# Weight parts in pair tiles: where the two parts of a split weight start in a partition

## The chip, the cores and the metric

The kernel runs on one core of one Trainium2 chip. The metric is the device time of one execution in microseconds, the median of several runs. The profile is one further execution, recorded by the hardware profiler; its span is the time from its first to its last instruction.

## The reference

Two decoder layers work on one sequence of 512 positions, with a width of 2048, in float32.

```python
for i in range(DEPTH):
    mod = (c_act @ ada_w[i] + ada_b[i])[:, None, :]
    shift, scale, gate = jnp.split(mod, 3, axis=-1)
    h = rmsnorm(x, norm_g[i]) * (1.0 + scale) + shift
    if i % N_MIXERS == 0:
        y = retention_branch(h, positions, ret_w_in[j], ret_gn_g[j], ret_w_out[j])
    else:
        y = mla_branch(h, positions, mla_w_in[j], ..., mla_w_out[j])
    x = x + gate * y
return rmsnorm(x, final_norm_g)
```

Layer 1 is a retention layer of 8 heads: `h @ w_in` gives queries and keys (256 columns a head each), values and gates (512 columns a head each); the branch output, gated, goes through `w_out` (4096 by 2048). Layer 2 is latent attention of 16 heads: an input projection to two latents of 512, a rotary key and a gate, up-projections of the latents, causal softmax attention, and an output projection (2048 by 2048).

## The kernel before

Everything is held transposed or in rows in tiles of 128 partitions. To keep float32 accuracy at the fast matmul format, every weight and activation is split in two parts of that format: hi, a cast by ScalarE (line 137, or in place at lines such as 846 and 850), and lo, the remainder, a subtraction by VectorE (line 138; 848, 851). A product is then three matmuls, hi x hi, hi x lo and lo x hi (`mm3`, lines 163 to 165, and lines 806 to 808 and 905 in the steps named below). TensorE thus runs some 11,000 matmuls of at most 128 by 128 by 512. In this document a matmul with 512 moving columns is called wide, one with 256 narrow.

A weight's way is: SyncE issues its load into a raw tile (three buffers of tag `raw`, three of `own_r`), ScalarE writes hi, VectorE writes lo, TensorE multiplies, and the tiles are free again. The hi and lo tiles are two separate tiles, from two rings of three buffers each (tags `whi` and `wlo`); a new tile takes a buffer of its ring that has come free. In the seven-product steps every fourth pair comes instead from a single extra pair (`own_h`, `own_l` in layer 1; two buffers `bm` in layer 2). Some weights use other rings (`k4b`, `big`).

The steps that the change touches:
- `plain_steps`: an ordinary product with a weight, three matmuls a block. Queries and keys of heads 1, 6 and 7 of layer 1 use it, as does the gate of layer 2 (`g2_steps`), whose first three units are worked in halves of 256 columns (line 1651).
- `seven_steps`: a product by seven block products in place of eight, for values and gates of heads 1 to 7 (tiles `vg...`) and for the two latents of layer 2. The weight parts are the moving operand, the activations and sums of them the stationary one. Units 0 to 7 of the first half (`vg_0..`) make products x, s, z, y with an even tile e and an odd tile o; the units of the second half (`vg_1..`) make x (with o), y (with e) and s (with o), in this order.
- `seven_rows_steps`: the same for queries and keys of heads 2 to 5 (tiles `qk_0..`, `qk_1..`) and for part of layer 2's gate, with the weight parts as the stationary operand and 256 moving columns (line 905).
- `o1_unit` and `o2_unit`: the output projections of the two layers (lines 1387 and 2309), wide for the most part, with some narrow units at their ends.

The order of the work on each engine is written out by the main loop over `steps`: loads three units ahead on SyncE's queue, the preparation (hi, lo) of the unit after the current one, the matmuls, and what follows; `behind` ties each engine's instructions to its last one. Within a unit the building layer decides the order on VectorE and ScalarE by when tiles come free. Modulation sums (line 1089) run on VectorE in between.

Tiles stand in SBUF one after another. A 32-byte tile `spacer` and the size of `qn_s` are chosen in the kernel before such that the operands of all wide and narrow matmuls start 64 bytes past a multiple of 128 in their partition.

Of the kernel before, what the change touches and what calls it, by code (L numbers as in the profile page):

```python
# [49 lines left out]
def hybrid_trunk_kernel(  # L50
# [71 lines left out]
    mhalf = base.tile([P, NT], F32, name="mhalf")  # L122
# [17 lines left out]
    def load_w(parts, a, b, name, later=None, where=None):  # L140
# [12 lines left out]
        return hi, lo  # L153
# [70 lines left out]
    a_col = [base.tile([P, KD], F32, name=f"a_col{i}") for i in range(2)]  # L224
    b_col = [base.tile([P, KD], F32, name=f"b_col{i}") for i in range(2)]
    gate_c = [base.tile([P, KD], F32, name=f"gate_c{i}") for i in range(2)]
# [92 lines left out]
    def first_load(kind, u):  # L319

        cn = 512
        tags = (("k4b", 4), ("k4b", 4)) if kind == "g" else (("whi", 3), ("wlo", 3))
        raw = big(f"{kind}0_{u}_raw", F32) if u == 0 else base.tile(
            [P, 2, cn], F32, tag="raw", bufs=3, name=f"{kind}0_{u}_raw"
        )
        c0 = {"v": 4096, "g": 8192}.get(kind)
        for dst, src in qk_parts(0, u) if kind == "qk" else [(whole, rows(w_ret_in, u, 2, c0, cn))]:
            nc.sync.dma_start(dst(raw), src)

        def prepare():  # L330
            hl = [base.tile([P, 2, cn], F32R, tag=t, bufs=n, name=f"{kind}0_{u}_{t}{i}") for i, (t, n) in enumerate(tags)]
# [377 lines left out]
    lpp = lp.__enter__()  # L709

# [27 lines left out]
    def plain_steps(nu, kn, parts, cn, name, take, n, lhs, rhs, evac, seeded=False, **kw):  # L738
# [3 lines left out]
        def step(u):  # L742
# [39 lines left out]
    def turns(raw_tags, part_tags):  # L782
# [12 lines left out]

        return raw_tile, part_tiles

    def seven_steps(h, block, form, raw_tile, part_tiles, finish, rows):


# [14 lines left out]
        def step(second, u):  # L815
# [14 lines left out]
            def prepare():  # L830
                e, o = w["e"], w["o"]
                if not second:
                    eh, el = part_tiles([P, 2, T], f"{n}e")
# [5 lines left out]
                    oh, ol = part_tiles([P, 2, T], f"{n}o")  # L839
# [4 lines left out]
                else:  # L844
                    oh, ol = part_tiles([P, 2, T], f"{n}o")
# [3 lines left out]
                    eh, el = part_tiles([P, T], f"{n}e")  # L849
# [37 lines left out]
    def seven_rows_steps(name, load_half, acts, sums, raw_tile, part_tiles, finish, rows):  # L887
# [30 lines left out]
        def step(second, u):  # L918
# [12 lines left out]
            def prepare():  # L931
                e, o = w["e"], w["o"]
                if not second:
                    e0, e1, o0, o1 = (t[:, :, j * H : (j + 1) * H] for t in (e, o) for j in range(2))
                    eh, el = part_tiles([P, 2, T], f"{n}e")
# [5 lines left out]
                    oh, ol = part_tiles([P, 2, T], f"{n}o")  # L941
# [4 lines left out]
                else:  # L946
                    oh, ol = part_tiles([P, 2, T], f"{n}o")
# [4 lines left out]
                    eh, el = part_tiles([P, T], f"{n}e")  # L952
# [36 lines left out]
    def heads_steps(h):  # L989
# [25 lines left out]
        ((lambda: lpp, ("own_h", "own_l"), 1), *3 * ((lambda: base, ("whi", "wlo"), 3),)),  # L1015
# [142 lines left out]
    def retention(h, own, own2=None):  # L1158
# [146 lines left out]
    for h in (6, 7):  # L1305
# [6 lines left out]
            ),  # L1312
# [54 lines left out]
    def o1_unit(n, r, u, kn, cn, where=(("whi", 3), ("wlo", 3))):  # L1367
# [85 lines left out]
    def second_out():  # L1453
        outs(2, range(4))
        for b in range(4):
# [6 lines left out]
            {4: 2 * (("big", 16),), 5: 2 * (("big", 16),), 6: 2 * (("k4b", 4),)}.get(u, (("whi", 3), ("wlo", 3))),  # L1462
# [157 lines left out]

    def l2_tile(tag, bufs, name, shape=(P, T), dt=F32):
        return pools["l2"].tile(list(shape), dt, tag=tag, bufs=bufs, name=name)
# [14 lines left out]
    ga = g2_steps(0, seeded=True)  # L1637
# [105 lines left out]
    qn_s = base.tile([P, 32], F32, name="qn_s")[:, :NT]  # L1743
# [25 lines left out]
    def latent_parts(n, g_c):  # L1769
# [11 lines left out]
    turns2 = turns(  # L1781
        ((lambda: pools["l2"], "bw", 2), (lambda: base, "raw", 3)),
        ((lambda: pools["l2"], ("bm", "bm"), 2), *3 * ((lambda: base, ("whi", "wlo"), 3),)),
    )
# [85 lines left out]
    def unit_prepare(kind, pr, u):  # L1870
        raw = unit_raw.pop((kind, pr, u))
        cn, tags = (384, (("whi", 3), ("wlo", 3))) if kind == "uq" else (512, 2 * (("k4b", 4),))
        hi, lo = unit_parts[kind, pr, u] = [
            base.tile([P, 2, cn], F32R, tag=t, bufs=n, name=f"{kind}_{pr}_{u}_{i}") for i, (t, n) in enumerate(tags)
        ]
# [70 lines left out]
    def attend(h):  # L1946
# [13 lines left out]
        def exps(i):  # L1960
            n = (i + 1) * P
            if i == 0:
# [194 lines left out]
    for i, step in enumerate(steps):  # L2157
        if i == n_p:
            lp.__exit__(None, None, None)
            l1 = tc.tile_pool(name="l1", bufs=1)  # L2160
            pools["l1"] = l1.__enter__()
        if i == n_l2:
            l1.__exit__(None, None, None)
            l2 = tc.tile_pool(name="l2", bufs=1)
            pools["l2"] = l2.__enter__()
        with behind(S_):
# [92 lines left out]
    def o2_unit(r, u, kn, cn, where=None):  # L2259
        wt = load_w([(whole, rows(w_mla_out, u, kn, r * T, cn))], kn, cn, f"o2_w{r}_{u}", where=where)  # L2260
# [212 lines left out]
```

## Time and profile before

| what | value |
|---|---|
| median of 3 runs | 2149.7 us (2149.39 to 2150.03) |
| the profiled execution's own time | 2149.59 us |
| its span | 2147.8 us |
| TensorE busy | 2122.6 us, 99% |
| VectorE busy | 1675.3 us, 78% |
| ScalarE busy | 1056.7 us, 49% |
| mean granted TensorE clock | 0.998 |

In the profile's rows PE is the matmuls of TensorE, PEld its weight loads, DVE VectorE, ACT ScalarE, SP SyncE. A row of a timeline has the start and the length in us, the engine, the line, the tiles (out<-in, buffer numbers left out), the shape and the count of merged instructions; in brackets, the idle time before it and what ended it. A row of a group has count, busy us and mean ns. Matmuls overlap each other, so a matmul's length is longer than the distance to the next one's start.

### The profile page before, as it was taken

Reading aid. Unit: us, or ns where it says so; the run is one execution under the profiler, and the core shown is the slowest. Engines: PE = TensorE matmul, PEld = TensorE weight load, DVE = VectorE, ACT = ScalarE, POOL = GpSimd, SP = SyncE. Lnnn points to the kernel's source line nnn. Section 1 sums busy time; section 2 is a strip of 40 time slices with the busy share of each in tenths; the row PEclk is TensorE's granted clock in tenths of the full one; section 3 lists DMA queues with packets and bytes.
Section 4 is the critical chain, followed back from the end, with each engine's and each line's share of the span. In section 5 each row is a group of like instructions: output and inputs, shape, how many; then the busy total and the mean of one; then the engine's idle time right before and its main releaser. Section 6 shows DMA issues by size and latency. Waiting matters only on the chain.

```text
span 2147.8 us, 30042 instructions
## 1 busy us (share of the span) xinstructions
PE 2122.6 (99%) x11100; PEld 1824.9 (85%) x11100; DVE 1675.3 (78%) x2482; ACT 1056.7 (49%) x1604; POOL 106.5 (5%) x178
## 2 busy tenths in 40 slices
PE   7999999999999999999999999999999999999998
PEld 5887898988889888888888888898889989988887
DVE  7899788888878789766777777668978788886745
ACT  5764444444444444434344544445446565664434
POOL 1000000000000000000000000010001000000000
PEclk9999999999999999999999999999999999999999
DMA  9976687877777778755647566553456644346734
GB/s 381 395 281 197 225 277 229 275 241 259 255 259 259 237 235 283 261 181 185 237 155 246 185 207 240 169 176 115 159 189 203 187 128 147 118 133 221 244 109 137
DMA packets 229782, 462.96 MB, mean 216 GB/s; under 512 B 20817, under 2 KB 84337, under 8 KB 225793
## 3 DMA queue, kind: packets, MB, share of 16 engines
q1 hardware_dynamic: 217424, 421.85, 59.6%
q0 software_dynamic: 11920, 38.91, 4.6%
q8 instruction: 87, 1.43, 0.3%
q14 instruction: 61, 0.50, 0.1%
q10 hardware_dynamic: 290, 0.27, 0.0%
HBM read 417.96 MB, written 43.00 MB: 215 GB/s over the span
## 4 chain that ended last, share of the span: by engine, by line
PE 82%; DVE 7%; DMA 5%; issue 2%; ACT 2%; POOL 1%; SPq 0%; DVEq 0%; POOLq 0%; ACTq 0%
PE o L1387 9%; PE o L2309 4%; PE x L806 2%; PE x L807 2%; PE y L806 2%; PE s L806 2%; PE x L808 2%; PE y L808 2%; PE s L808 2%; PE s L807 2%; PE y L807 2%; PE y_qk L905 2%; PE s_qk L905 2%; PE x_qk L905 2%; DMA mod<-in_ada_t_dram 2%
## 5 line engine op out<-in xcount | busy, mean ns | idle before, releaser
L1387 PE MATMUL o<-o_h,o_whi 128*128 128x512 f32 (+1 forms) x496 | 192.3, 388 | 0.0
L1387 PE MATMUL o<-o_h,o_wlo 128*128 128x512 f32 (+1 forms) x496 | 191.9, 387 | 0.1
L1387 PE MATMUL o<-o_l,o_whi 128*128 128x512 f32 (+1 forms) x496 | 191.3, 386 | 0.0
L1387 PEld LDWEIGHTS o<-o_h,o_wlo 128*128 128x128 f32 x496 | 93.2, 188 | 20.1 <-DVE o_wlo L138 1.5
L138 DVE TENSOR_TENSOR o_wlo<-o_r,o_whi 128x1024 fp32r<-128x1024 f32 x61 | 74.5, 1223 | 44.1 <-ACT o_whi L137 43.5
L1387 PEld LDWEIGHTS o<-o_h,o_whi 128*128 128x128 f32 x496 | 93.2, 188 | 18.2
L1387 PEld LDWEIGHTS o<-o_l,o_whi 128*128 128x128 f32 x496 | 93.2, 188 | 18.2
L165 PE MATMUL qk<-hT,qk_l 128*128 128x512 f32 x192 | 74.8, 390 | 1.5 <-DVE qk_l L138 1.5
L358 DVE SCALAR_TENSOR_TENSOR aw<-aw,c_all 128x2048 f32<-128x2048 f32 (+1 forms) x35 | 73.0, 2101 | 2.7 <-DMA aw<-in_ada_t_dram 2.6
L163 PE MATMUL qk<-hT,qk_h 128*128 128x512 f32 x192 | 75.0, 391 | 0.0
L164 PE MATMUL qk<-hT,qk_h 128*128 128x512 f32 x192 | 74.7, 389 | 0.0
L1089 DVE SCALAR_TENSOR_TENSOR mod<-mod,c_odd 128x1024 f32<-128x1024 f32 x48 | 58.0, 1220 | 20.1 <-DMA mod<-in_ada_t_dram 20.1
L137 ACT CAST o_whi<-o_r 128x1024 fp32r<-128x1024 f32 x61 | 63.4, 1051 | 20.8 <-PE o L1387 18.4
L138 DVE TENSOR_TENSOR o_w_lo<-o_w_raw,o_w_hi 128x1024 fp32r<-128x1024 f32 x32 | 38.9, 1220 | 32.7 <-ACT o_w_hi L137 32.6
L1089 DVE SCALAR_TENSOR_TENSOR mod<-mod,c_bm 128x1024 f32<-128x1024 f32 x48 | 58.5, 1219 | 0.0
L2309 PE MATMUL o<-o_h,o_w_hi 128*128 128x512 f32 (+1 forms) x160 | 55.6, 348 | 0.0
L2309 PE MATMUL o<-o_h,o_w_lo 128*128 128x512 f32 (+1 forms) x160 | 55.5, 347 | 0.0
L2309 PE MATMUL o<-o_l,o_w_hi 128*128 128x512 f32 (+1 forms) x160 | 55.4, 347 | 0.0
L1242 ACT ACTIVATE yn<-y,nmr,gn_r 128x512 f32<-128x512 f32 x32 | 22.3, 778 | 62.0 <-DVE nmr L1236 62.0
L137 ACT CAST o_w_hi<-o_w_raw 128x1024 fp32r<-128x1024 f32 x32 | 33.5, 1050 | 36.3 <-PE o L2309 32.5
L164 PE MATMUL o<-o_l,o_w_hi 128*128 128x512 f32 x128 | 50.1, 391 | 0.5 <-DVE o_l L138 0.5
L137 ACT CAST o_h<-o_in 128x1024 fp32r<-128x1024 f32 x24 | 25.2, 1052 | 51.1 <-PE o L164 47.2
(1608 smaller groups left out, 6893.4 us busy)
## 6 DMA issues: line engine op xcount, KB each, us to landing
mod<-in_ada_t_dram SPq DMA_DIRECT2D x96, 512.0 KB, 5.8
o_r<-in_ret_w_out_dram SPq DMA_DIRECT2D x64, 512.0 KB, 5.3
aw<-in_ada_t_dram SPq DMA_DIRECT2D x30, 1024.0 KB, 9.0
mod_gate<-in_ada_t_dram SPq DMA_DIRECT2D x32, 512.0 KB, 5.0
o_w_raw<-in_mla_w_out_dram SPq DMA_DIRECT2D x32, 512.0 KB, 4.0
qk_r<-in_ret_w_in_dram SPq DMA_DIRECT2D x48, 256.0 KB, 3.2
qk_r<-qk_d SPq DMA_DIRECT2D x32, 256.0 KB, 5.7
v_r<-v_d SPq DMA_DIRECT2D x32, 256.0 KB, 6.2
```

The source lines that it names most:

```text
L137: ACT.copy(hi, src)
L138: DVE.tensor_sub(lo, src, hi.bitcast(F32))
L163: PE.matmul(o, lhs[0], rhs[0], start=first and not seeded, stop=False, skip_group_check=seeded)
L164: PE.matmul(o, lhs[0], rhs[1], start=False, stop=False, skip_group_check=seeded)
L165: return PE.matmul(o, lhs[1], rhs[0], start=False, stop=last, skip_group_check=seeded)
L806: PE.matmul(banks[b], a[0], w[0], start=first, stop=False, skip_group_check=True)
L807: PE.matmul(banks[b], a[0], w[1], start=False, stop=False, skip_group_check=True)
L808: PE.matmul(banks[b], a[1], w[0], start=False, stop=True, skip_group_check=True)
L905: PE.matmul(o, w[wp][:, i, b * P : (b + 1) * P], a[ap], start=first and i + b + k == 0, stop=k == 2, skip_group_check=True,)
L1089: DVE.scalar_tensor_tensor(out=aw, in0=aw, scalar=1.0, in1=silu_c[j], op0=ALU.mult, op1=ALU.mult, accum_out=mc[:, j, b : b + 1],)
L1387: PE.matmul(o, w[i][:, ki, c0 + b * P : c0 + (b + 1) * P], a[j], start=first and i + j == 0, stop=last and i == 1, skip_group_check=True,)
L2309: PE.matmul(banks2[b][:, cols], w[0][i][:, 0, b * P : (b + 1) * P], o2_moving(w, u, cols)[j], start=u + i + j == 0, stop=u == KD - 1 and i ...
```

## The change

The hi and lo parts that came from `whi` and `wlo` now stand in one pair tile: 2 x 1024 elements and 16 spare ones, which are 64 bytes. There are three pair tiles in the base pool, and one more in the pool of layer 1's projections and one in that of layer 2. The three are dealt in a fixed turn (`next_pair`); in the seven-product steps every fourth pair is the extra one. hi starts `at` elements into the pair and lo 1024 elements after it:
- `EVEN`, 16 elements (64 bytes): such that a part starts 64 bytes past a multiple of 128, as all other operands do;
- `ASIDE`, 0: on a multiple of 128. It is used where a weight part meets narrow matmuls as the stationary operand: `seven_rows_steps`, the halved units of layer 2's gate, the narrow units of the output projections that use pair tiles;
- 12, 8 and 4 elements (48, 32 and 16 bytes) for values and gates of heads 2, 4 and 6, and for queries and keys of heads 1, 6 and 7. With these the parts start 48, 32 and 16 bytes past a multiple of 128; the other operand of these matmuls starts where it did.

Space for it comes from small tiles: `rt` and `mhalf` share one tile, `spacer` and its memset go, `qn_s` is halved, the statistics tile `st6` becomes one of the `small` ring. In layer 2's attention the probabilities of every second head stand in the extra pair in place of two `bm` tiles.

```diff
-    rt = base.tile([P, 4], F32, name="rt")
-    spacer = base.tile([P, 8], F32, name="spacer")
-    DVE.memset(spacer, 0.0)
...
-        where = where or (("whi", 3), ("wlo", 3))
-        hi, lo = (
-            base.tile([P, a, b], F32R, tag=tag, bufs=n, name=f"{name}_{p}") for p, (tag, n) in zip(("hi", "lo"), where)
-        )
+        hi, lo = two_tiles(where, [P, a, b], name, ASIDE if halved else EVEN)
...
+    EVEN, ASIDE = 16, 0
+
+    def pair_tile(pool, tag, name):
+        return pool.tile([P, 2 * 1024 + EVEN], F32R, tag=tag, bufs=1, name=name)
...
+    def next_pair(name):
+        i = n_pairs[0] % 3
+        n_pairs[0] += 1
+        return ready.pop(i, None) or pair_tile(base, f"pair{i}", name)
+
+    def parts_of(pair, shape, at):
+
+        n = math.prod(shape[1:])
+        views = [pair[:, 1024 * i + at : 1024 * i + at + n] for i in range(2)]
+        return views if len(shape) == 2 else [v.rearrange("p (k n) -> p k n", k=shape[1]) for v in views]
+
+    def two_tiles(where, shape, name, at=EVEN):
+
+        if where is None:
+            return parts_of(next_pair(name), shape, at)
+        return [base.tile(list(shape), F32R, tag=t, bufs=n, name=f"{name}_{i}") for i, (t, n) in enumerate(where)]
...
-                w["hl"] = [
-                    base.tile([P, kn, cn], F32R, tag=tag, bufs=3, name=f"{name}_{u}_{tag[1]}") for tag in ("whi", "wlo")
-                ]
+                w["hl"] = two_tiles(None, [P, kn, cn], f"{name}_{u}_p", ASIDE if u < halved else EVEN if at is None else at)
...
-        def part_tiles(shape, name):
+        def part_tiles(shape, name, at):
             n[1] += 1
-            pool, tags, bufs = part_tags[n[1] % len(part_tags)]
-            return [pool().tile(shape, F32R, tag=tag, bufs=bufs, name=f"{name}_{p}") for p, tag in zip("hl", tags)]
+            return parts_of(next_pair(name) if n[1] % 4 else own(name), shape, at)
...
     def seven_steps(h, block, form, raw_tile, part_tiles, finish, rows):

+        at = {2: 12, 4: 8, 6: 4}.get(h, EVEN)
...
-                    oh, ol = part_tiles([P, 2, T], f"{n}o")
+                    oh, ol = part_tiles([P, 2, T], f"{n}o", at)
...
-                    eh, el = part_tiles([P, 2, T], f"{n}e")
+                    eh, el = part_tiles([P, 2, T], f"{n}e", ASIDE)
...
-                sums=lambda u: {0: 2, 1: 3, 2: 4, 4: 5, 5: 6, 6: 7}.get(u),
+                sums=lambda u: {0: 2, 1: 3, 2: 4, 4: 5, 5: 6, 6: 7}.get(u), at=12,
...
-                st = l1_tile("st6", 4, f"st_{h}_{i}", (P, 6))
+                st = small(f"st_{h}_{i}", 6)
...
-            ),
+            ), at={6: 8, 7: 4}[h],
...
-            hl = [base.tile([P, kn, cn], F32R, tag=t, bufs=b, name=f"o1_{n}_{r}_{u}_{t}{i}") for i, (t, b) in enumerate(where)]
+            hl = two_tiles(where, [P, kn, cn], f"o1_{n}_{r}_{u}_p", ASIDE if kn == 1 and u > 3 else EVEN)
...
-    ga = g2_steps(0, seeded=True)
+    ga = g2_steps(0, seeded=True, halved=3)
...
-                    both = [l2_tile("bm", 2, f"p_{h}_{j}", (P, 2, T)) for j in range(2)]
-                    p_.extend(both[j // 2][:, j % 2, :] for j in range(NT))
+                    both = l2_pair(f"p_{h}_").bitcast(F32)
+                    p_.extend(both[:, j * T : (j + 1) * T] for j in range(NT))
...
+        halved = kn == 1 and u >= KD - 4
+        wt = load_w([(whole, rows(w_mla_out, u, kn, r * T, cn))], kn, cn, f"o2_w{r}_{u}", where=where, halved=halved)
```

More of the change, by code (lines that the diff above doesn't have):

```diff
@@ L121, in hybrid_trunk_kernel @@
     DVE.memset(ones, 1.0)
-    mhalf = base.tile([P, NT], F32, name="mhalf")
+    few = base.tile([P, 2 * NT], F32, name="few")
+    rt, mhalf = few[:, :NT], few[:, NT:]
     DVE.memset(mhalf, -0.5)
-    rt = base.tile([P, 4], F32, name="rt")
-    spacer = base.tile([P, 8], F32, name="spacer")
-    DVE.memset(spacer, 0.0)
     def rsqrt(src, n, mul, name):
@@ L138, in split, with load_w @@
         DVE.tensor_sub(lo, src, hi.bitcast(F32))
-    def load_w(parts, a, b, name, later=None, where=None):
+    def load_w(parts, a, b, name, later=None, where=None, halved=False):
         raw = base.tile([P, a, b], F32, tag="raw", bufs=3, name=f"{name}_raw")
@@ L222, in hybrid_trunk_kernel @@
     final_c = vcol[:, 168:184]
[L224 to L226 removed]
+    EVEN, ASIDE = 16, 0
+    def pair_tile(pool, tag, name):
+        return pool.tile([P, 2 * 1024 + EVEN], F32R, tag=tag, bufs=1, name=name)
+    a_col, b_col, gate_c, ready, n_pairs = [], [], [], {}, [0]
+    for i in range(3):
+        ready[i] = pair_tile(base, f"pair{i}", f"pair_{i}")
+        if i < 2:
+            for cols, name in ((a_col, "a_col"), (b_col, "b_col"), (gate_c, "gate_c")):
+                cols.append(base.tile([P, KD], F32, name=f"{name}{i}"))
+    def next_pair(name):
[10 more added lines that the diff above has]
+        return [base.tile(list(shape), F32R, tag=t, bufs=n, name=f"{name}_{i}") for i, (t, n) in enumerate(where)]
     def modulate(i, ps_shift, ps_scale, k0, n):
@@ L321, in first_load @@
         cn = 512
-        tags = (("k4b", 4), ("k4b", 4)) if kind == "g" else (("whi", 3), ("wlo", 3))
+        where = (("k4b", 4), ("k4b", 4)) if kind == "g" else None
         raw = big(f"{kind}0_{u}_raw", F32) if u == 0 else base.tile(
@@ L330, in prepare @@
         def prepare():
-            hl = [base.tile([P, 2, cn], F32R, tag=t, bufs=n, name=f"{kind}0_{u}_{t}{i}") for i, (t, n) in enumerate(tags)]
+            hl = two_tiles(where, [P, 2, cn], f"{kind}0_{u}_p")
             ACT.copy(hl[0], raw)
@@ L709, in hybrid_trunk_kernel @@
     lpp = lp.__enter__()
+    own_ready = [pair_tile(lpp, "own", "own_pair")]
     def keep_rows(ps, dst_d, r0, name, func=AF.Identity, own=None):
@@ L736, in __init__, with plain_steps @@
             self.beside = {"load": [], "form": [], "multiply": []}
-    def plain_steps(nu, kn, parts, cn, name, take, n, lhs, rhs, evac, seeded=False, **kw):
+    def plain_steps(nu, kn, parts, cn, name, take, n, lhs, rhs, evac, seeded=False, halved=0, at=None, **kw):
         banks = {}
@@ L1014, in hybrid_trunk_kernel @@
         ((lambda: lpp, "own_r", 3), (lambda: base, "raw", 3)),
-        ((lambda: lpp, ("own_h", "own_l"), 1), *3 * ((lambda: base, ("whi", "wlo"), 3),)),
+        lambda name: own_ready.pop() if own_ready else pair_tile(lpp, "own", name),
     )
@@ L1619, in hybrid_trunk_kernel, with l2_pair @@
     rotary2, kr = [], {}
+    l2_ready = []
+    def l2_pair(name):
+        return l2_ready.pop() if l2_ready else pair_tile(pools["l2"], "own", name)
     def l2_tile(tag, bufs, name, shape=(P, T), dt=F32):
@@ L1871, in unit_prepare @@
         raw = unit_raw.pop((kind, pr, u))
[L1872 to L1875, printed above, removed]
+        cn, where = (384, None) if kind == "uq" else (512, 2 * (("k4b", 4),))
+        hi, lo = unit_parts[kind, pr, u] = two_tiles(where, [P, 2, cn], f"{kind}_{pr}_{u}_p")
         if kind == "ukv":
@@ L2165, in hybrid_trunk_kernel @@
             pools["l2"] = l2.__enter__()
+            l2_ready.append(pair_tile(pools["l2"], "own", "own_pair2"))
         with behind(S_):
```

27 lines of the change are left out of this document (12 added, 15 removed).

## The prediction

> **What bounds the kernel now.** I read the page first, then TensorE's waits, then stretches of its timeline, because only the timeline shows how far apart two matmuls start. The page's engine row, slices and chain:
>
> ```profile
> PE 2122.6 (99%) x11100; PEld 1824.9 (85%) x11100; DVE 1675.3 (78%) x2482; ACT 1056.7 (49%) x1604; POOL 106.5 (5%) x178
> PE   7999999999999999999999999999999999999998
> PEclk9999999999999999999999999999999999999999
> PE 82%; DVE 7%; DMA 5%; issue 2%; ACT 2%; POOL 1%; SPq 0%; DVEq 0%; POOLq 0%; ACTq 0%
> ```
>
> TensorE is busy 99% of the span, the granted clock is full in every slice, and the chain of waits is 82% TensorE. TensorE's largest waits:
>
> ```profile
> PE xT_ps L435 <- DVE x_diag L525: 3.4, 4, 1.4
> ...
> PE s L163 <- ACT yn L1242: 1.0, 4, 0.3
> ```
>
> The largest is 3.4 us, at the start. So the time is the number of matmuls times the distance between their starts; nothing else can move it by more than a few us unless it starves TensorE. (A row's own length, 0.39 or 0.28 us, is no distance: consecutive matmuls overlap.)
>
> The distances, from TensorE's timeline (start, length, line, tiles, count). First wide matmuls (512 columns) in a steady stream, then narrow ones (256 columns):
>
> ```profile
> 396.20 0.39 PE L806 MATMUL x<-vg_17o_h,hT 128*128 128x512 f32 x1
> ...
> 399.37 0.39 PE L808 MATMUL y<-vg_17e_h,sums 128*128 128x512 f32 x1
> 399.60 0.40 PE L905 MATMUL x_qk<-hT,qk_00e_h 128*128 128x256 f32 x2
> 399.83 0.28 PE L905 MATMUL x_qk<-hT,qk_00e_l 128*128 128x256 f32 x1
> ...
> 401.03 0.40 PE L905 MATMUL s_qk<-sums,qk_00e_h 128*128 128x256 f32 x2
> ...
> 405.23 0.28 PE L905 MATMUL y_qk<-sums,qk_00o_l 128*128 128x256 f32 x1
> ```
>
> Wide: 14 steps in 3.17 us, 226.4 ns each. Narrow: 35 steps in 4.20 us, 120.0 ns. The difference, 106.5 ns for 256 columns, is 0.416 ns a column, so 213 and 106.5 ns are columns and some 13.4 ns are added to either. Both distances are near whole multiples of 6.67 ns (34 and 18), half of what is added. I call 6.67 ns a beat; that streams settle on it is my reading of these two numbers.
>
> Away from the steady stream the same shapes go at other rates:
>
> ```profile
> 1701.47 0.40 PE L163 MATMUL uq<-qT,uq 128*128 128x512 f32 x1
> ...
> 1702.86 0.39 PE L163 MATMUL uq<-qT,uq 128*128 128x512 f32 x1
> ...
> 1724.03 0.40 PE L163 MATMUL uq<-qT,uq 128*128 128x512 f32 x1
> 1724.27 0.39 PE L164 MATMUL uq<-qT,uq 128*128 128x512 f32 x1
> 1724.49 0.40 PE L165 MATMUL uq<-qT,uq 128*128 128x512 f32 x1
> ...
> 1727.05 0.38 PE L1958 MATMUL a<-kr,qr 128*128 128x128 f32 x2
> 1727.27 0.34 PE L163 MATMUL a<-ukT,uqT 128*128 128x256 f32 x1
> 1727.45 0.28 PE L164 MATMUL a<-ukT,uqT 128*128 128x256 f32 x1
> ...
> 1727.92 0.34 PE L163 MATMUL a<-ukT,uqT 128*128 128x384 f32 x1
> ```
>
> Six wide steps take 1.39 us, 231.7 ns each; single ones 240 and 220. Four narrow ones take 0.47 us, 117.5 ns; the two at 399.60 took 0.23, 115 each. 128-column ones, which spend little on columns, still need 110 ns. So off the steady rhythm wide matmuls are slower and narrow ones faster than in it. The rates are not fixed by the number of columns, and something in how operands are read can move them.
>
> **The change part by part.** No matmul, cast or subtraction is added; one 128x8 memset of VectorE goes. No DMA is added or changes its queue. TensorE's and POOL's lists keep their order; ScalarE's, VectorE's and SyncE's have local swaps.
>
> *Stationary parts aside, narrow matmuls.* Before, both operands of every wide and narrow matmul start 64 bytes past a multiple of 128 in their partition. After, the stationary weight part of most narrow ones starts on the multiple, the moving one stays. The counts, from rows that take the whole span as one stretch, for L905, L1651 and L806 in this order (TensorE busy and count, weight loads busy and count), and a group's row:
>
> ```profile
> 0.00:2148.00 2148.00, 243.17 (x2016) 242.69 (x2016) 1.00 0.65 216
> ...
> 0.00:2148.00 2148.00, 17.97 (x144) 17.50 (x144) 1.00 0.65 216
> ...
> 0.00:2148.00 2148.00, 348.60 (x896) 168.22 (x896) 1.00 0.65 216
> ...
> L163 PE MATMUL qk<-hT,qk_h 128*128 128x512 f32 x192 | 75.0, 391 | 0.0
> ```
>
> All 2016 of L905 and 144 of L1651 move, and by the built program's addresses 48 at L1387 and 96 at L2309: 2304. No row before has such a pair of starts, so the price is bounded: below by the 110 ns of the 128-column rows (-10 x 2304 = -23.0 us), above by one beat (+15.4 us), as nothing excludes a loss. If a steady stream can only rest on whole beats, a changed rate is 113.3 or 126.7 ns; the rows off the rhythm (115, 117.5) lie on the lower side. I take 113.3: 2304 x -6.67 = **-15.4 us**.
>
> *Parts at 16, 32 and 48 bytes, wide matmuls.* Heads 2, 4 and 6 of values and gates have their moving part there: 896 a line is 8 groups of 112, so 3 x 112 x 3 lines = 1008. The plain queries and keys of heads 1, 6 and 7 have their stationary part there: the 192 are all three heads of one line, times 3 lines = 576. Together 1584. One more stretch of wide ones off the rhythm, ten steps:
>
> ```profile
> 1722.88 0.39 PE L163 MATMUL a<-ukT,uqT 128*128 128x512 f32 x1
> ...
> 1725.18 0.39 PE L165 MATMUL uq<-qT,uq 128*128 128x512 f32 x1
> ```
>
> That is 230.0 ns a step. The floor is columns alone (-13.4 x 1584 = -21.2 us); the ceiling is the 240 ns row (+13.4 x 1584 = +21.2 us). The nearest rows are the two off-rhythm stretches, 231.7 and 230.0; I take 4.3 ns above the steady rate, about their middle: 1584 x 4.3 = **+6.8 us**.
>
> *A rule against both terms.* The Trainium skill, "TensorE: Matmul & The Clock Gate", section "Step-by-step: what each phase is for", gives the two operands independent read ports: "Loading the next tile's weights doesn't steal SBUF read bandwidth from the running matmul." By that rule both terms are zero and the sum is that of the second rival; the trace only partly agrees, since equal shapes run at 226.4 and 231.7 ns, and no run so far shows why.
>
> *Pairs with fixed places.* Before, hi and lo parts came from rings of three, and a part took whichever slot came free; after, places are dealt in a fixed turn. In the second half of a head's values, the odd tile is used first and last in a unit (products x and s), the even one in between (y). Before, every second unit crossed over, in ScalarE's and VectorE's rows:
>
> ```profile
> 386.24 1.05 ACT L846 CAST vg_16o_h<-vg_16o_r 128x1024 fp32r<-128x1024 f32 x1 [1.67 <-PE y L808]
> 387.56 0.62 ACT L850 CAST vg_16e_h<-vg_16e_r 128x512 fp32r<-128x512 f32 x1 [0.26 <-PE s L808]
> 387.33 1.22 DVE L848 TENSOR_TENSOR vg_16o_l<-vg_16o_r,vg_16o_h 128x1024 fp32r<-128x1024 f32 x1 [0.94 <-ACT vg_16o_h L846]
> 389.07 0.68 DVE L847 TENSOR_TENSOR vg_17e_r<-vg_17o_r,vg_17e_r 128x512 f32<-128x512 f32 x1
> ...
> 391.67 0.39 PE L807 MATMUL x<-vg_16o_l,hT 128*128 128x512 f32 x1
> ```
>
> Unit 6's odd cast waited for y of two units before; now it waits for s, as its even cast did, 387.56 - 386.24 = 1.32 us later. Behind it the 1.22 us subtraction now queues after the next unit's 0.68. Its lo was done at 388.55 and TensorE took it at 391.67: 3.12 us of cover less 1.32 and 0.68 leaves 1.1 us, so I cost it at nothing. Without the cover (a 1.22 us modulation sum in front as well) it is about 0.1 us in each of 3 units of 7 heads, 2 us, and TensorE then waits for the lo part. The odd units already ran so. Attention's second head now keeps its four probability tiles in one pair instead of two tiles: a later start of its exponentials, covered by the other head's work. The small statistics tiles move to a common ring; the existing wait s <- yn may grow by 0.1 us in each of its 4 places: **+0.4 us**.
>
> *Cover under faster narrow matmuls.* The stretch 415 to 450 us is mostly narrow ones. Its row (length, then busy us and count of TensorE, its weight loads, VectorE, ScalarE, POOL, then clock, DMA share, GB/s):
>
> ```profile
> 415.00:450.00 35.00, 35.00 (x254) 33.26 (x254) 29.50 (x41) 14.85 (x19) 2.87 (x4) 1.00 0.85 285
> ```
>
> VectorE works 29.5 of 35 us and DMA engines 0.85. With 5.6% less TensorE time these become 89% and 0.90: still under TensorE. I allow **+0.6 us**; if transfers were the next to be late, the gain of the L905 stretches (2016 x 6.67 = 13.4 us) would shrink towards nothing.
>
> *The sum.* -15.4 + 6.8 + 0.4 + 0.6 = -7.6 us on the profiled execution's own 2149.6 us (span 2147.8 and 1.8 around it), which is the median 2149.7 within 0.1: **2142 us**.
>
> **The rivals.**
> - *Wide parts off the steady start cost a beat, narrow ones gain nothing* (slower). For it: every stretch off the rhythm is slower for wide matmuls, and nothing steady shows narrow ones below 120. One beat on 1584 is 10.6 us: 2161 us. It decides from 4.3 us on, 2.7 ns a wide matmul with no narrow gain. Against it: narrow rows off the rhythm were faster.
> - *Starts don't matter, the change does not do what it says* (the independent ports of the page named above): only the 0.4 us remain, 2150 us. For it: tiles at many different places all show the same distance.
> - *Both terms are only of off-rhythm size*: 2304 x -2.5 = -5.8 and +6.8, with the 1.0: 2151.6 us.
> - *Stationary parts aside cost narrow ones a beat*: +15.4 us with wide ones unchanged, 2165 us. Against it: no narrow stretch is slower than 120.
>
> **How the numbers follow.** About 0.2%, 4.3 us, is what can be told from no change here. The forecast (narrow ones a beat faster, wide ones losing less than that) has 0.41; its own range is 2134 to 2146, from wide unchanged to wide losing all of a beat. The wide loss alone 0.27, starts that don't matter 0.14, both small 0.10, the narrow loss 0.08. Faster is then 0.41, within 0.2% 0.24, slower 0.35. The range takes the forecast's low end, 2134, and reaches over the wide loss with a little more than a beat, 2163; the narrow loss and narrow matmuls at 110 ns lie outside.
>
> **What would show it.** Right: L905 narrow steps near 113 ns where they were 120; the wide steps of the vg heads 2, 4, 6 near 231 while heads 3, 5, 7 stay at 226; no TensorE wait over 1 us in the value stretches. Wrong: narrow steps at 120 or more; wide ones at 233 or above for one of the three distances, or below 226; a new wait of x at L806 or L807 for VectorE's lo part.

## The result, and the profile after

The changed kernel takes 2155.0 us (median, 2153.73 to 2156.66) against 2149.4 for the kernel before in the same session (2147.50 to 2150.96). The ratio is 1.0026 with a 95% interval of 1.0018 to 1.0035: slower by 5.6 us, between 3.9 and 7.5. The forecast was 2142, faster. The profiled execution took 2153.73 us, with a span of 2151.9; before it was 2147.8, so the two traces differ by 4.1 us.

The page of the changed kernel, engine row, granted clock and chain:

```profile
PE 2124.8 (99%) x11100; PEld 1817.6 (84%) x11100; DVE 1677.1 (78%) x2481; ACT 1054.3 (49%) x1604; POOL 106.6 (5%) x178
PEclk9999999999999999999999999999999999999999
PE 84%; DVE 6%; DMA 5%; issue 2%; ACT 2%; POOL 1%; SPq 0%; DVEq 0%; POOLq 0%; ACTq 0%
```

TensorE is still the bound at full clock. Three of its waits:

```profile
PE c_ps L455 <- DMA c_all<-in_c_dram: 3.2, 1, 3.2
PE xT_ps L455 <- DVE x_diag L545: 2.8, 4, 1.1
...
PE s L158 <- ACT yn L1261: 1.1, 3, 0.4
```

The 17 rows sum to 17.4 us, the 14 of before to 15.8. None is at lines 825 to 827 or at 924 (806 to 808 and 905 before), where most of the change lies. So 1.6 us are waits, in small pieces, and the rest has to be in the distances between starts.

A distance is best read by counting. A row for a stretch that holds nothing but one kind of matmul gives its start and end, its length, and then TensorE's busy time with the number of matmuls that touch the stretch (behind them clock, DMA share and GB/s); the length plus one matmul's own length (0.39 us wide, 0.28 narrow), divided by that number, is the distance. One matmul more or less moves it by 0.7 ns (wide) or 0.4 (narrow). The kernel before, values of head 1, then queries and keys of head 2:

```profile
207.63:277.63 70.00, 70.00 (x310) 1.00 0.75 245
283.79:321.79 38.00, 38.00 (x319) 1.00 0.81 269
```

That is 70.39/310 = 227.1 ns wide and 38.28/319 = 120.0 narrow; the prediction had 226.4 and 120.0. The kernel after, in this order: values of heads 1 (64 bytes), 2 (48), 4 (32) and 6 (16); plain queries and keys of heads 1 (48), 6 (32) and 7 (16); the narrow L924 of head 2; and the halved gate, L1675 (L1651 before):

```profile
207.08:277.08 70.00, 70.00 (x310) 1.00 0.76 248
322.81:397.81 75.00, 75.00 (x323) 1.00 0.73 233
556.67:631.67 75.00, 75.00 (x323) 1.00 0.73 233
750.91:825.91 75.00, 75.00 (x321) 1.00 0.77 254
164.21:204.21 40.00, 40.00 (x178) 1.00 0.54 170
905.94:941.94 36.00, 36.00 (x156) 1.00 0.72 238
...
1006.90:1016.90 10.00, 10.00 (x45) 1.00 0.35 116
...
283.24:321.24 38.00, 38.00 (x325) 1.00 0.85 286
1458.50:1467.50 9.00, 9.00 (x82) 1.00 0.03 12
```

| matmuls | start, bytes past a multiple of 128 | ns before | ns after | count | us |
|---|---|---|---|---|---|
| values, head 1 | moving 64 | 227.1 | 227.1 | | 0 |
| values, head 2 | moving 48 | 227.1 | 233.4 | 336 | +2.1 |
| values, head 4 | moving 32 | 227.1 | 233.4 | 336 | +2.1 |
| values, head 6 | moving 16 | 227.1 | 234.9 | 336 | +2.6 |
| plain qk, head 1 | stationary 48 | 227.1 | 226.9 | 192 | 0 |
| plain qk, head 6 | stationary 32 | 227.1 | 233.3 | 192 | +1.2 |
| plain qk, head 7 | stationary 16 | 227.1 | 230.9 (to 5 ns) | 192 | +0.7 |
| narrow, L924 | stationary 0 | 120.0 | 117.8 | 2016 | -4.4 |
| narrow, the other three lines | stationary 0 | 120.0 | 113.2 at L1675, taken for all three | 288 | -1.9 |

The rates sum to +2.4 us and the waits to +1.6: 4.0 of the 4.1 us between the two traces. That fit is closer than its parts. Both traces hold the same 11100 matmuls in the same order, so the steps from each start to the next can be added up by kind: the narrow matmuls come to -5.8 us (L924 -4.4, the other three lines -1.4), the shifted wide ones to +9.1, and all else, waits included, to +0.8. The narrow matmuls did get faster, but those of L924 by a third of what was forecast; most of the shifted wide ones lost about a beat of 6.67 ns where I had put 4.3 ns, and those with a stationary part at 48 bytes lost nothing.

### The profile page after: what moved, and what is told of

It is laid out like the page before. It is cut to its first block, busy times and chain, and to the rows that moved or that the text cites. A ratio compares the mean times of both kernels' runs of the same rounds, so it can differ in the third digit from the quotient of the medians.

```text
span 2151.9 us, 29960 instructions
## 1 busy us (share of the span) xinstructions
PE 2124.8 (99%) x11100; PEld 1817.6 (84%) x11100; DVE 1677.1 (78%) x2481; ACT 1054.3 (49%) x1604; POOL 106.6 (5%) x178
## 4 chain that ended last, share of the span: by engine, by line
PE 84%; DVE 6%; DMA 5%; issue 2%; ACT 2%; POOL 1%; SPq 0%; DVEq 0%; POOLq 0%; ACTq 0%
PE o L1406 11%; PE o L2331 4%; PE x L826 2%; PE x L827 2%; PE s L826 2%; PE s L827 2%; PE y L826 2%; PE x L825 2%; PE y L827 2%; PE s L825 2%; PE y L825 2%; PE x_qk L924 2%; PE s_qk L924 2%; PE y_qk L924 2%; PE qk L160 2%
## 5 line engine op out<-in xcount | busy, mean ns | idle before, releaser
L1406 PE MATMUL o<-o_h,o_p 128*128 128x512 f32 (+1 forms) x1088 | 323.1, 377 | 0.0
L1406 PEld LDWEIGHTS o<-o_h,o_p 128*128 128x128 f32 x1088 | 199.9, 188 | 37.4 <-DVE o_p L136 0.3
L1406 PE MATMUL o<-o_l,o_p 128*128 128x512 f32 (+1 forms) x544 | 204.9, 377 | 0.0
L1406 PEld LDWEIGHTS o<-o_l,o_p 128*128 128x128 f32 x544 | 102.3, 188 | 18.3
L136 DVE TENSOR_TENSOR o_p<-o_r,o_p 128x1024 fp32r<-128x1024 f32 x64 | 78.1, 1223 | 50.4 <-ACT o_p L135 49.9
L2331 PE MATMUL o<-o_h,o_w 128*128 128x512 f32 (+1 forms) x320 | 82.1, 346 | 0.0
L135 ACT CAST o_p<-o_r 128x1024 fp32r<-128x1024 f32 x64 | 66.5, 1051 | 27.1 <-PE o L1406 15.0
L160 PE MATMUL qk<-hT,qk_p 128*128 128x512 f32 x192 | 75.4, 393 | 1.5 <-DVE qk_p L136 1.5
L158 PE MATMUL qk<-hT,qk_p 128*128 128x512 f32 x192 | 75.8, 395 | 0.0
L159 PE MATMUL qk<-hT,qk_p 128*128 128x512 f32 x192 | 75.4, 393 | 0.0
L2331 PEld LDWEIGHTS o<-o_h,o_w 128*128 128x128 f32 x320 | 55.9, 188 | 7.5
L158 PE MATMUL o<-o_h,o_w 128*128 128x512 f32 x128 | 50.1, 391 | 0.0
L160 PE MATMUL o<-o_h,o_w 128*128 128x512 f32 x128 | 49.9, 390 | 0.0
```

The source lines that it names most:

```text
L135: ACT.copy(hi, src)
L136: DVE.tensor_sub(lo, src, hi.bitcast(F32))
L158: PE.matmul(o, lhs[0], rhs[0], start=first and not seeded, stop=False, skip_group_check=seeded)
L159: PE.matmul(o, lhs[0], rhs[1], start=False, stop=False, skip_group_check=seeded)
L160: return PE.matmul(o, lhs[1], rhs[0], start=False, stop=last, skip_group_check=seeded)
L1406: PE.matmul(o, w[i][:, ki, c0 + b * P : c0 + (b + 1) * P], a[j], start=first and i + j == 0, stop=last and i == 1, skip_group_check=True,)
```

## The experiments

Theory at the start: the shifted starts cost the wide matmuls about a beat, the aside starts give L924 only a third of one, and the pairs with fixed places cost what the rates leave over, 2.4 us. Rivals: the loss is new waits from the fixed places; the narrow gain is hidden behind late parts; a start costs by where it lies and not by its distance to the other operand's.

**The change in its parts.** Three kernels, each the changed kernel with parts undone: e1_no_shift has the first edit below (and EVEN for the plain queries and keys of heads 1, 6 and 7), e3_shift_only the second, e2_pairs_only both.

```diff
-    at = {2: 12, 4: 8, 6: 4}.get(h, EVEN)
+    at = EVEN
...
-    EVEN, ASIDE = 16, 0
+    EVEN, ASIDE = 16, 16
```

> Undoes the shifts alone: every wide weight part starts 64 bytes past a multiple of 128 again, pairs and fixed places stay, narrow stationary parts stay aside. Theory (the shifts cost a beat, the aside starts give less than a beat): the 1584 shifted wide matmuls go back from 233 to 227 ns, 336 x 8 + 672 x 6.6 + 192 x 5.2 + 192 x 6.5 = 9.4 us less than the changed kernel's 2155.0, so 2145.6, faster than before by 3.8. Rival (the loss is new waits from the fixed places, the rates only look different): it stays within 2 us of the changed kernel, 2153 or more.

> Pairs and fixed places alone: every weight part, those of narrow matmuls too, starts at 64. Theory: all rates are those of before (227 and 120), and what the pairs cost by themselves is what the rates leave over of the changed kernel's 5.6 us: -6.2 for the narrow ones and +9.4 for the shifted wide ones make +3.2, so +2.4 is left, 2151.8. Rival one (the order of the places is free, as I had it at 0.4 us): 2149.4 to 2149.8. Rival two (the narrow gain is not due to the start but to the pairs): L924 keeps 117.8 ns here too and the time is 2145 to 2146.

> Pairs and the shifts to 16, 32 and 48 bytes, but the narrow matmuls' stationary parts at 64 again. Theory: 6.2 us more than the changed kernel, 2161.2; L924 back at 120.0 ns, the shifted wide ones at 233 to 235. Rival (the narrow gain of 2.2 ns a matmul is hidden behind late weight parts and transfers in those stretches): the same time as the changed kernel, 2155.

| kernel | median us | ratio to before | 95% interval |
|---|---|---|---|
| e1_no_shift | 2146.0 | 0.9980 | 0.9971 to 0.9990 |
| e2_pairs_only | 2151.0 | 1.0003 | 0.9994 to 1.0012 |
| e3_shift_only | 2161.6 | 1.0052 | 1.0036 to 1.0067 |
| the change | 2155.0 | 1.0026 | 1.0018 to 1.0035 |

Against 2149.7 us, the ratios say: pairs alone +0.6 (-1.3 to +2.6), the aside starts -4.9 more (e2 to e1), the shifts +9.9 more (e1 to the change). The theory holds for the shifts and the aside starts; pairs with fixed places cannot be told from no change, nor from the 2.4 us, but they are not the loss, so the rival of new waits is out. Nor do the pairs make the narrow gain: in e2 the L924 of head 2 is at 120.0 ns. The narrow gain is not hidden: without it (e3) the time is 6.6 us longer by the medians, 5.6 by the ratios. One thing was unexpected. In e3 the values of head 2, at the same addresses as in the changed kernel, run slower than there:

```profile
284.45:322.45 38.00, 38.00 (x319) 1.00 0.85 285
324.76:399.76 75.00, 75.00 (x318) 1.00 0.72 229
```

75.39/318 = 237.1 ns, where the changed kernel has 233.4; 336 x 3.7 = 1.2 us of e3's extra time are these. What differs is the stream in front of them, narrow matmuls at 120.0 ns and not 117.8.

**A table of starts.** e4_sweep gives each head its own start (the plain queries and keys too, at 0, 8 and 56 bytes).

```diff
-    at = {2: 12, 4: 8, 6: 4}.get(h, EVEN)
+    at = {1: 0, 2: 1, 3: 2, 4: 6, 5: 10, 6: 14, 7: 15}.get(h, EVEN)
...
+    at = {"qk2": 4, "qk3": 8, "qk4": 12, "qk5": 14, "g22": 2, "g23": 1}.get(name, ASIDE)
```

> A table of starts in one run. Moving weight parts of the values' heads 1 to 7 start at 0, 4, 8, 24, 40, 56 and 60 bytes past a multiple of 128 and the latent group's at 64; stationary parts of the plain queries and keys of heads 1, 6, 7 at 0, 8, 56; stationary parts of the narrow groups qk2 to qk5, g22, g23 at 16, 32, 48, 56, 8, 4. Theory (a row is read in pieces of 64 bytes, 6.67 ns each, and a row that does not start on a multiple of 64 needs one piece more): wide moving at 4 to 60 bytes all near 233.3 ns, at 0 as at 64, 226.7; narrow ones 120 or more at all of 4 to 56. Rival one (the cost depends on the distance of the two starts): the steps differ among 4 to 60 bytes by more than 3 ns. Rival two (pieces of 128 bytes): wide moving at 0 is a beat or two faster than 226.7, at 220 or 213.

The stretches of the values' heads 1 to 7, moving at 0, 4, 8, 24, 40, 56 and 60 bytes (first 0, last 60), and of the plain queries and keys of head 1 (stationary at 0) and the narrow qk2 (16), qk4 (48), g22 (8):

```profile
207.26:282.26 75.00, 75.00 (x323) 1.00 0.76 242
324.87:399.87 75.00, 75.00 (x314) 1.00 0.71 224
447.11:517.11 70.00, 70.00 (x302) 1.00 0.72 227
562.50:637.50 75.00, 75.00 (x322) 1.00 0.73 233
680.72:755.72 75.00, 75.00 (x323) 1.00 0.72 232
759.12:829.12 70.00, 70.00 (x305) 1.00 0.77 249
837.13:907.13 70.00, 70.00 (x310) 1.00 0.74 246
...
164.00:204.00 40.00, 40.00 (x176) 1.00 0.53 170
285.66:321.66 36.00, 36.00 (x311) 1.00 0.86 288
523.08:559.08 36.00, 36.00 (x309) 1.00 0.86 292
1631.49:1669.49 38.00, 38.00 (x319) 1.00 0.62 180
```

Wide, moving: 233.4, 240.1, 233.1, 234.1, 233.4, 230.8 and 227.1 ns. Wide, stationary at 0: 229.5. Narrow: 116.7, 117.4 and 120.0. The theory of 64-byte pieces falls: moving at 0 is a multiple of 64 and costs a whole beat. Pieces of 128 bytes fall too, as 0 is slower and not faster. What is left of the three is the first rival, that the price depends on the distance between the two operands' starts. With the stationary operand at 64, a moving part at 64 or 60 bytes costs nothing, one at 56 half a beat, one from 8 to 48 or at 0 about a beat, one at 4 two beats. The whole kernel took 2163.0 us (one run).

**The place or the distance.** e5_all_on moves everything by 32 bytes (on top of e1_no_shift).

```diff
-    few = base.tile([P, 2 * NT], F32, name="few")
+    few = base.tile([P, 4 * NT], F32, name="few")
```

> The kernel with no shifts (wide parts at 64, narrow stationary parts at 0) with 32 more bytes in one small tile ahead of everything: every wide operand now starts at 96, narrow moving ones at 96 and stationary ones at 32, so all distances between two operands' starts are as they were. Theory (only the distance of the two starts counts): wide 226.7 and narrow 117.8 ns as without the 32 bytes, 2146.0. Rival (the place itself counts, 64 bytes being the piece that is read): all 13,000 us of wide rows' starts are off a multiple of 64, wide matmuls rise to 230 or more in every stretch, over 2160.

(The "13,000 us" there is a slip; the rival is that all wide matmuls slow down.) Measured: 2146.7 us, ratio 0.9985 (0.9976 to 0.9995), which cannot be told from e1_no_shift. Values of head 1, and narrow qk2:

```profile
207.01:277.01 70.00, 70.00 (x310) 1.00 0.75 242
283.17:321.17 38.00, 38.00 (x325) 1.00 0.87 292
```

227.1 and 117.8 ns, both operands at 96 or at 96 and 32. For these distances the place itself does not count; the other distances were not moved this way.

**Why 117.8 at L924 and 113.2 at L1675.** The two have the same starts, 64 and 0. L924 writes the two halves of one bank in turn and ends its accumulation after each three; L1675 goes through four banks and does not. e6_orders changes these in L924 by group, on top of e1_no_shift.

```diff
+        if name == "qk5": terms = ((0, 0), (1, 0), (0, 1))
+        if name == "qk4": turn = [(i, b, k) for b in range(2) for i in range(2) for k in range(3)]
+        if name == "g22": turn = [(i, b, k) for i in range(2) for k in range(3) for b in range(2)]
...
-    stop=k == 2
+    stop=j == len(turn) - 1 if name == "qk3" else k == 2
```

> Same addresses as the kernel with no shifts; the narrow groups differ in the order of their matmuls. qk2 and g23 as before; qk3 ends its accumulation after twelve matmuls and not after each three; qk4 does six matmuls on one half of the bank before the other half; qk5 takes the weights hi, lo, hi in place of hi, hi, lo; g22 changes the half after each matmul; the 144 of g2_0 at the start of the latent layer get an end after each three. Theory (the two rates, 113.3 and 117.8, are two rhythms that the same addresses can fall into, and how the stream was entered decides): qk2, g23 and qk3 stay at 117.8; g2_0 still shows stretches of both rates; qk4, qk5 or g22 may fall into another rhythm, anywhere from 113.3 to 120. Rival one (the end mark costs 13.3 ns a group of three): qk3 goes to 114.4 and g2_0 to 117.8 throughout. Rival two (changing the half of one bank costs it): qk4 goes to 115.6, g22 above 120.

Narrow qk3 (one end), qk4 (one half six times), qk5 (hi, lo, hi):

```profile
401.23:439.23 38.00, 38.00 (x325) 1.00 0.87 290
...
517.10:555.10 38.00, 38.00 (x325) 1.00 0.87 293
...
632.91:670.91 38.00, 38.00 (x325) 1.00 0.87 295
```

All at 38.28/325 = 117.8, and g22, which changes the half each time, is at 117.8 too. The halved gate (g2_0), now with its ends, still begins at 113.3. Both rivals fall: neither the end mark nor the halves make the difference. What precedes the stream is the next candidate. The whole kernel took 2148.4 us (one run).

**Other starts for the narrow ones.** On top of e1_no_shift, e7_narrow_16 puts L924's parts at 16 bytes (the first edit, at all four places where `ASIDE` stands), and e8_apart gives hi and lo different starts (the second).

```diff
-    eh, el = part_tiles([P, 2, T], f"{n}e", ASIDE)
+    eh, el = part_tiles([P, 2, T], f"{n}e", 4)
...
-    views = [pair[:, 1024 * i + at : 1024 * i + at + n] for i in range(2)]
+    ats = at if isinstance(at, tuple) else (at, at)
+    views = [pair[:, 1024 * i + ats[i] : 1024 * i + ats[i] + n] for i in range(2)]
```

> The kernel with no shifts, and the 2016 narrow stationary parts of L924 at 16 bytes in place of 0. Theory (the distance 48 gives 116.7 ns in every group as it did in one): 2016 x 1.1 = 2.2 us less than with 0, 2143.8, faster than before by 6. Rival (the 116.7 was the one group's own entry): other groups at 117.8 or above, 2146 or more.

> The kernel with no shifts, the hi and the lo part of a pair at different starts (hi, lo in bytes). Values' heads 1 to 7: 0 and 64, 32 and 64, 60 and 64, 56 and 64, 48 and 64, 16 and 64, 60 and 60; plain queries and keys of heads 1, 6, 7: 32 and 64, 0 and 64, 48 and 64; narrow groups qk2 to qk5, g22, g23: 0 and 16, 0 and 32, 16 and 64, 0 and 64, 16 and 32, 32 and 48. Of three matmuls two use the hi part. Theory (each matmul's own distance sets its price): a mixed wide group costs two thirds of the price of its hi start, near 231.1 ns for 0, 32 and 48; the narrow ones lie between the rates of their two starts, 116.7 to 118.5. Rival (the price arises between neighbours in the stream, where the distance changes): wide groups with two starts above 233.3, or narrow ones at 113.3 as in the streams where stationary parts at 0 and 64 take turns.

e7_narrow_16: 2143.8 us, ratio 0.9972 (0.9962 to 0.9982), and all six groups at 116.7 as the theory had it. e8_apart: 2157.7 us (one run). Its values of head 1 (0 and 64), head 2 (32 and 64), head 3 (60 and 64) and head 5 (48 and 64), and narrow qk2 (0 and 16):

```profile
212.00:282.00 70.00, 70.00 (x300) 1.00 0.74 229
330.00:400.00 70.00, 70.00 (x302) 1.00 0.72 230
447.00:517.00 70.00, 70.00 (x307) 1.00 0.72 230
690.00:760.00 70.00, 70.00 (x304) 1.00 0.73 234
290.00:320.00 30.00, 30.00 (x257) 1.00 0.82 268
```

234.6, 233.1, 229.3, 231.5 and 117.8 ns. At 0, 32 and 48 bytes two thirds of a beat was expected, 231.1; head 5 shows it, heads 1 and 2 pay as much as if all their parts were shifted. Head 3 pays 2 ns although neither of its starts costs anything alone. So a matmul's own distance does not set its price by itself; that the price arises between neighbours, as the rival has it, fits these rows but is not shown. The rival's 113.3 for narrow matmuls did not come, and the narrow row here lies inside the theory's range and decides nothing.

**The entry.** Each L924 group follows wide matmuls. The halved gate, L1675, begins behind narrow ones at 64. Its first 34 matmuls, then its last 94 behind a wait, in the changed kernel, and the same 94 in e1_no_shift:

```profile
1449.51 4.02 PE L1675 MATMUL g<-h,g_p 128*128 128x256 f32 x34
...
1457.22 10.99 PE L1675 MATMUL g<-h,g_p 128*128 128x256 f32 x94 [0.35 <-ACT h L1528]
...
1449.86 11.39 PE L1675 MATMUL g<-h,g_p 128*128 128x256 f32 x94 [0.35 <-ACT h L1528]
```

The 34 go at (4.02 - 0.28)/33 = 113.3 ns, in e1_no_shift too. The 94 average 115.2 ns in the changed kernel and 119.5 in e1_no_shift; past a few longer steps behind the wait they settle at 113.3 and at 117.8, with the same starts and the same matmuls just in front. e9_entry leaves the first even tile of five groups at 64, on top of e1_no_shift.

```diff
-    eh, el = part_tiles([P, 2, T], f"{n}e", ASIDE)
+    eh, el = part_tiles([P, 2, T], f"{n}e", EVEN if u == 0 and name != "qk3" else at)
...
-    ga = g2_steps(0, seeded=True, halved=3)
+    ga = g2_steps(0, seeded=True, halved=8)
```

> The kernel with no shifts; in five of the six narrow groups the very first even weight tile (24 of 336 matmuls) keeps 64, so that the stream reaches the aside starts through narrow matmuls at 64 and not straight from wide ones; the rest is at 0 in qk2 and g22, 16 in qk4, 32 in qk5, 48 in g23. qk3 is left as it was (all at 0). Beside it the wide matmuls of g2_0 (120) get their stationary part at 0, behind narrow ones at 0. Theory (the entry decides which of two rhythms the same addresses run in): qk2 and g22 run at 113.3 ns behind their first 24, qk3 at 117.8; the groups at 16, 32 and 48 bytes may change too. The wide ones of g2_0, entered from narrow ones, run at another rate than the 228.9 that was seen behind wide ones. Rival (the line's own pattern of halves and addresses sets the rhythm): 117.8 in qk2 and g22 too, 116.7 at 16 and 32, and 228.9 for the wide ones.

TensorE's timeline as it goes into qk2, 24 matmuls at 64 and then the first at 0 (line 924 is 926 in this kernel):

```profile
283.07 0.39 PE L827 MATMUL y<-vg_17e,sums 128*128 128x512 f32 x1
283.29 1.60 PE L926 MATMUL x_qk<-hT,qk_00e 128*128 128x256 f32 x12
284.73 1.60 PE L926 MATMUL s_qk<-sums,qk_00e 128*128 128x256 f32 x12
286.17 1.07 PE L926 MATMUL z_qk<-hT,qk_00o 128*128 128x256 f32 x8
```

24 steps from 283.29 to 286.17 are 120.0 ns each. Then qk2 and, as left, qk3; and g22 early and late:

```profile
286.87:316.87 30.00, 30.00 (x267) 1.00 0.85 284
398.83:436.83 38.00, 38.00 (x325) 1.00 0.88 289
...
1617.81:1627.81 10.00, 10.00 (x91) 1.00 0.39 109
1632.12:1652.12 20.00, 20.00 (x172) 1.00 0.75 225
```

qk2 runs at 30.28/267 = 113.4 ns from the first matmul at 0 to its end; qk3, entered from wide ones, at 117.8. g22 begins at 10.28/91 = 113.0 and goes on at 117.9. Between the two a weight load waits for a lo part:

```profile
1631.19 1.24 PEld L926 LDWEIGHTS x_g<-h,g_03e 128*128 128x128 f32 x10 [0.29 <-DVE g_03e L961]
```

So with the same starts, and in qk2 and qk3 the same line and pattern, there are two steady rates. Entered from narrow matmuls at 64 the stream takes the faster, entered from wide ones the slower: that is the theory, shown. A short pause can throw a stream from the faster into the slower; L1675 shows that it need not, and what decides there stays open. The theory's side claim missed: the wide ones of g2_0 at 0 kept the rate that stationary starts at 0 had behind wide ones. Groups at 16 and 32 bytes kept 116.7, and the one at 48 bytes fell to 120. The whole kernel took 2144.2 us (one run).

**Both, and the change with the entry.** e10_both is e1_no_shift with an entry in every group and one more in g22 and g23, where the pause falls; e11_change_entry is the changed kernel with the same line.

```diff
-    eh, el = part_tiles([P, 2, T], f"{n}e", ASIDE)
+    eh, el = part_tiles([P, 2, T], f"{n}e", EVEN if u == 0 or u == 3 and name[0] == "g" else ASIDE)
```

> The kernel with no shifts, every narrow group entered through a first even tile at 64; g22 and g23, where a pause of TensorE falls into the fourth unit, go through one more at the start of that unit. 192 of the 2016 narrow matmuls stay at 64, the other 1824 at 0. Theory (113.3 ns holds from the entry on): against the kernel with no shifts 1824 x 4.44 = 8.1 us less, 192 x 2.2 = 0.4 more, 7.7 in all from its 2146.0: 2138.3, a ratio of 0.9945 to before. Rival (weight parts and transfers cannot follow at 5.6% less TensorE time, so the gain shrinks to new waits): 2141 or more, with waits of TensorE for a cast or a transfer over 1 us at L924.

> The changed kernel, shifts at 16, 32 and 48 bytes and all, with only that entry added. Theory: 7.7 us less than the changed kernel's 2155.0, 2147.3, which is 2 to 3 us faster than before instead of slower: the sign of the result hung on the rhythm of L924. Rival (its 5.6 us come from the shifts and from order, and the entry does little in their company): 2152 or more.

e10_both: 2139.7 us (2137.50 to 2140.62), ratio 0.9955 (0.9942 to 0.9969), faster than both kernels, by 9.1 us than the one before on the same chip (2148.7). Queries and keys of head 2, the end of g23, which fell back to 118.2 ns, and the wide matmuls behind head 2's narrow ones:

```profile
286.30:316.30 30.00, 30.00 (x267) 1.00 0.82 270
1679.74:1689.74 10.00, 10.00 (x87) 1.00 0.37 110
...
322.80 0.39 PE L827 MATMUL s<-vg_00e,sums 128*128 128x512 f32 x1
323.34 0.47 PE L825 MATMUL s<-vg_00e,sums 128*128 128x512 f32 x1 [0.15 <-DVE m_qk L1070]
```

No wait of TensorE stands at L924, so parts and transfers kept up there. But the product s right behind each of the four groups of queries and keys now starts 0.3 us late, for a sum that VectorE has not finished. Added up from the starts of the two traces, L924 gains 6.9 us against e1_no_shift, and the values behind it give 1.5 back, 0.4 in each of the four stretches. The 5.4 that are left are what the ratios show, where 7.7 were expected. e11_change_entry: 2149.7 us, ratio 1.0006 (0.9997 to 1.0015): no difference from before that can be told. Against the changed kernel that is 5.3 us less by the medians and 4.3 by the ratios, where 7.7 were expected. By the starts of both traces L924 again gains 6.9 us; but the values of head 2, entered now from the faster narrow stream, went from 233.4 to 237.1:

```profile
324.60:399.60 75.00, 75.00 (x318) 1.00 0.70 229
```

With the late product s in front, 1.4 us are given back there, and 1.1 in the other three stretches behind narrow matmuls. That leaves 4.4, as the ratios have it.

## Why the prediction was wrong

**What bounds the kernel** held: TensorE at 99% and full clock, and the time is the distances: of the 4.1 us between the two traces, those of the narrow and the shifted wide matmuls make 3.3.

**Stationary parts aside** (-15.4 us) is the step that failed. "If a steady stream can only rest on whole beats, a changed rate is 113.3 or 126.7 ns" was wrong in its premise: L924 rests at 117.8, which is between 17 beats (113.3) and 18 (120.0). The same addresses can run at 113.3, as L1675 and e9_entry show, but no L924 stream that came straight from wide matmuls got there. The term measured -5.8 us by the starts, or -4.9 by e2 to e1. My bounds (-23.0 to +15.4) held it; the value I took was the better of two rhythms, and the row nearest to it off the rhythm, 117.5, would have been right.

**Parts at 16, 32 and 48 bytes** (+6.8 us) had the right sign and a wrong size. 4.3 ns on every one of 1584 was in fact 6.3 to 7.8 for moving parts, 6.2 for stationary ones at 32, some 4 at 16 and nothing at 48: +9.1 us by the starts, +9.9 by e1 to the change. That is a whole beat for most, which the rival "wide parts off the steady start cost a beat" had as its mechanism, at 10.6.

**Pairs with fixed places** (+0.4 us) was not contradicted: +0.6, between -1.3 and +2.6. The steps went as described. After the change, ScalarE's row of the odd cast in values of head 2, VectorE's of its lo part and TensorE's first with that part (the second of each three takes it) are:

```profile
388.16 1.05 ACT L865 CAST vg_16o<-vg_16o_r 128x1024 fp32r<-128x1024 f32 x1 [0.78 <-PE s L827]
389.24 1.22 DVE L867 TENSOR_TENSOR vg_16o<-vg_16o_r,vg_16o 128x1024 fp32r<-128x1024 f32 x1 [0.53 <-ACT vg_16o L865]
392.35 0.39 PE L826 MATMUL x<-vg_16o,hT 128*128 128x512 f32 x1
```

The cast waits for s, as foreseen; lo is done at 390.46, and TensorE takes it 1.89 us later, where I had worked out 1.1 us of cover. No wait of x arose.

**Cover under faster narrow matmuls** (+0.6 us) was not called on in the changed kernel, whose L924 runs at 117.8. In e10_both, at the full speed, the cover does fail, not at L924 but in the product s behind it, and costs 1.5 us.

**The sum.** -15.4 + 6.8 + 1.0 became -5.8 + 9.1 + 0.8. Of the miss of 13 us, 9.6 are the first term and 2.3 the second; the medians lie another 1.5 further apart than the two traces. With the first term that small, the second outweighs it, and a forecast of faster became slower. The time lies within the stated range, closest to the third rival (both terms of off-rhythm size, 2151.6), which had a chance of 0.10 and whose narrow rate of 117.5 is nearly what L924 has.

**The rule on independent ports** (Trainium skill, "TensorE: Matmul & The Clock Gate", section "Step-by-step: what each phase is for") would have given no change in either term. The runs disagree as far as rates go: moving the stationary part alone takes a narrow matmul from 120.0 to 117.8, and wide ones from 227.1 to 233.3, while moving both by the same 32 bytes changes nothing. Which part of the chip this comes from is not shown here; for the two distances that were moved as a whole, it goes by the distance of the two starts, and why is open.

## What to carry to other kernels

Where TensorE is the bound, count the matmuls in a pure stretch for each pair of operand starts before and after any change of layout: here a part that moved by 16 bytes cost 3% of a wide matmul, and one that moved by 64 gained 2 to 5.5% of a narrow one. A steady rate belonged to a stream and to how it was entered, so a rate seen in one place is a candidate for another and not a forecast; try it in place, and if a better rhythm is known, lead the stream into it. When two terms of opposite sign are both of the size of a guess, the sign of their sum is not known, and a run of each alone says more than a finer sum.

## What the runs showed that I had not expected

- Two steady rates at the same starts and in the same line: 113.4 and 117.8 ns (qk2 and qk3 of e9_entry), chosen by the matmuls in front. Behind a pause L1675 ran at either, and why is open. Wide ones at 48 bytes ran at 233.4 behind narrow ones at 117.8 ns, and at 237.1 behind narrow ones at 120.0 and at 113.4.
- A wait of 0.29 us for a lo part cost more than itself: what followed in g22 ran 4.5 ns a matmul slower.
- Moving parts at 0 are a beat slower than at 64 (233.4 against 227.1) when the stationary part stays at 64, though both are multiples of 64; at 4 bytes it is two beats (240.1), at 60 none.
- Shifts of at most 64 bytes decide 23 us, from 2139.7 (e10_both) to 2163.0 (e4_sweep, one run), with the same matmuls in nearly the same order.
